# Normalising and transposing rows under the modulation weights' load, modulating three blocks at a time, and updating mLSTM states inside each head's projection

## The chip, the core and the metric

The kernel runs on one core of a Trainium2 chip. Its engines work side by side and meet through semaphores: TensorE (PE, with its weight loads listed as PEld), VectorE (DVE), ScalarE (ACT), GpSimd (POOL), and SyncE (SP), whose queue issues nearly all DMAs. The metric is the device time of one execution in microseconds, lower is better; a kernel's time is the median of several runs.

## The reference

One transformer layer over 128 context tokens (block 0) and 1024 latent tokens (blocks 1 to 8), width 1024. The layer reads attention and a bidirectional mLSTM from one input projection, merges them, and ends with a SwiGLU network. Everything is float32.

```python
def trunk_layer(x, mods, ...):
    sh1, sc1, g1, sh2, sc2, g2 = mods              # split of silu(cond) @ w_ada + b_ada
    h = rmsnorm(x, norm1_w) * (1 + sc1) + sh1
    aq, ak, av, mq, mk, mv, mo, mg = jnp.split(h @ w_in, SPLIT_POINTS, axis=-1)
    ...                                            # q/k norms, rotary
    attn_o = attention(aq, keys, vals)
    hm, st_f, st_b = mlstm_bidir(heads(mq), heads(mk) * (MLSTM_DK ** -0.5), heads(mv), gates, init_f, init_b)
    hm = (rmsnorm(hm, mlstm_norm_w) * jax.nn.sigmoid(mo))
    x = x + g1 * (jnp.concatenate([attn_o, hm], axis=-1) @ w_out)
    h2 = rmsnorm(x, norm2_w) * (1 + sc2) + sh2
    x = x + g2 * swiglu(h2, w_gu, w_down)

def step(carry, inp):                              # one mLSTM chunk of 128 tokens, per head and direction
    ...
    num = s @ vc + inter[..., None] * (qc @ C)
    C_new = decay[..., None, None] * C + jnp.einsum('bhs,bhsd,bhse->bhde', w, kc, vc)
    n_new = decay[..., None] * n + jnp.einsum('bhs,bhsd->bhd', w, kc)
```

The context rows are modulated with one condition and the latent rows with another. The latent scans start from given states; the context block starts from zero, and its states after one chunk are outputs.

## The kernel before

Tokens are nine blocks of 128 rows; three blocks form a chunk of 384 columns. A float32 operand is split into a high and a low part, so a product is three matmuls: high by high, high by low, low by high. The first projection uses float16 parts under a power-of-two scale that is taken from bounds on the features (`hsc`) and on the weights (`Scaled`).

The order that the code is written in is a list of priorities. A planner with a model of the engines' times orders each engine's instructions from it; `hot(n)` raises the priority of what stands in it. Generators are advanced against each other by `weave` (main against side steps) and `beside` (several sides, each with its own rate).

The stages, with their lines:

1. *Loads and modulation* (L265 to L377). SP's queue loads x block 0, then 16 pieces of the modulation weight (`aw`, 512 KB each). `strip_products` (L323) multiplies them with silu(cond); `cols_from_strips` (L329) turns the result into per-feature columns `shift1` and `scale1`. Both are then scaled per partition by `hsc` (L372 to L377). The key/value/gate columns of `w_in` (`kraw`, L444) and the other x blocks (L445 to L448) load after the modulation weights.
2. *Features* (L457 to L493). Per block: `normalise` (squares on ACT, reciprocal root in short DVE operations, scaling), eight transposes into PSUM (`transposed`, L344), then modulation straight from PSUM in eight 128x128 pieces (L470 on ACT, L473 on DVE) into float32 `full`; the high half is a cast (L479 on ACT, L481 on DVE), the low half a subtraction (L482, its instruction at L136, mostly on POOL). Side work: `ada`, the rest of the modulation weights, and `steps`, the bounds of the query weights.
3. *Keys, values, gates* (`linear_tok` with `evac_kvg`, L529), whose products the planner starts as features come.
4. *Query projection* (L965), with `gate_work` at rate 0.25, `ada` at 0.8, `kwork` at 0.8 and `steps` at 0.3 beside it. `gate_work` turns the gates into decay factors and the columns `QT` that the scans use; the part behind L579 waits ten side steps.
5. *Heads* (L1400 to L1405). `head_project(h)` makes queries (three chunks, L771) and then per block keys, values and output gates (L514 to L516, 384 columns; `evac` L749). `head_mlstm(h - 1)`, the scan of the head before, runs beside it at rate 0.67, attention at about 0.1. A scan first walks both directions in turn (L792 to L826): weight the values (`weighted`, POOL, on DVE in the last head), one 128x129 product with the keys (L813), one DVE update of the state (L823). Then it goes through the blocks (L847 to L890): products with queries and states (L834, L857, L864), a sum, a division by the normaliser (L867 to L878), and POOL multiplications (L881, L887).
6. *Last scan* (L1410), beside the first half of the output projection (`first`), the last modulation (`ada`) and attention.
7. Prefill, the feed-forward network and the finish follow (L1433 on).

## Time and profile before

| | us |
|---|---|
| median of 3 runs | 1625.65 |
| lowest and highest | 1624.38, 1627.73 |
| the profiled execution, its time | 1626.38 |
| the profiled execution, its span | 1624.6 |

The mean granted TensorE clock is 0.971 of full speed. The span is the time from the first to the last instruction of the profiled execution. A row of a group gives line, engine, operation, the output tile and its inputs, shapes and count, then the busy time and the mean time of one in ns, then the idle time of the engine just before them and what ended it. A row of the timeline gives start, duration, engine, line and operation, and in brackets the idle time before it and what released it. A row of the stages gives the stretch, its length, and per engine the busy time and the number of instructions, then the granted clock, the DMA engines' share and their rate. An instruction of PE that follows another closely overlaps it, so its duration is longer than its share of the engine.

### The profile page before, as it was taken

The page shows a single profiled execution, that of the slowest core. Times are in us where ns is not written, and L with a number is a line of the kernel's source. Part 1 is how long each engine was busy: PE and PEld are TensorE (multiplying, and loading weights), DVE is VectorE, ACT ScalarE, POOL GpSimd, SP SyncE. Part 2 cuts the span into 40 slices and gives each one's busy share as a digit, 9 for nine tenths or more (in the row PEclk, how much of TensorE's full clock was granted, in tenths as well). Part 3 has the DMA queues.
Part 4 walks back from the last instruction along what each step waited for, and adds up shares of the span by engine and source line. Part 5 has one row for each costly group of instructions (what it writes and reads, how often), then busy time and mean ns, then how long its engine had stood idle before and what let it go on. Part 6 is the DMA issues. An engine that isn't in the chain of part 4 may idle for free. (4 is left out here: it accounts for less than half of the span.)

```text
span 1624.6 us, 23438 instructions
## 1 busy us (share of the span) xinstructions
PE 1507.5 (93%) x8592; PEld 1254.6 (77%) x8592; DVE 937.6 (58%) x1895; ACT 755.6 (47%) x1373; POOL 657.5 (40%) x507
## 2 busy tenths in 40 slices
PE   5888899999988679999999999899999999999996
PEld 2644566667666467889999899798898989899995
DVE  3877745737657566556642646767674564333445
ACT  3754456756545444535433344565562443333232
POOL 0443332424241433544345354433434454545443
PEclk8899999999988899999999999999999999999998
DMA  9564232533447545867753546787774445545441
GB/s 356 184 178 128 83 71 49 112 50 66 103 108 175 184 141 124 211 167 169 174 153 114 149 146 212 188 181 170 163 171 131 132 142 173 157 130 149 129 142 68
DMA packets 387882, 236.92 MB, mean 146 GB/s; under 512 B 170199, under 2 KB 346791, under 8 KB 387767
## 3 DMA queue, kind: packets, MB, share of 16 engines
q1 hardware_dynamic: 385110, 231.84, 53.7%
q10 hardware_dynamic: 2656, 3.58, 0.7%
q8 instruction: 68, 1.11, 0.3%
q14 instruction: 48, 0.39, 0.1%
HBM read 183.79 MB, written 13.26 MB: 121 GB/s over the span
## 5 line engine op out<-in xcount | busy, mean ns | idle before, releaser
L136 POOL TENSOR_TENSOR wlo<-raw,whi 128x1024 fp32r<-128x1024 f32 (+1 forms) x144 | 352.0, 2448 | 419.3 <-ACT whi L153 387.9
L153 ACT CAST whi<-raw 128x1024 fp32r<-128x1024 f32 (+1 forms) x216 | 221.6, 1026 | 403.9 <-DMA raw<-in_w_gu_dram 160.4
L1305 PE MATMUL mm<-aTl,whi 128*128 128x384 f32 x1056 | 355.1, 336 | 0.0
L1304 PE MATMUL mm<-aTh,whi 128*128 128x384 f32 x1056 | 354.0, 336 | 0.9 <-DVE tn L1323 0.9
L1306 PE MATMUL mm<-aTh,wlo 128*128 128x384 f32 x1056 | 354.6, 336 | 0.0
L1304 PEld LDWEIGHTS mm<-aTh,whi 128*128 128x128 f32 x1056 | 198.2, 188 | 2.2 <-DVE tn L1323 1.5
L1306 PEld LDWEIGHTS mm<-aTh,wlo 128*128 128x128 f32 x1056 | 198.4, 188 | 1.5 <-issue 1.3
L1305 PEld LDWEIGHTS mm<-aTl,whi 128*128 128x128 f32 x1056 | 198.4, 188 | 0.8
L136 DVE TENSOR_TENSOR wlo<-raw,whi 128x1024 fp32r<-128x1024 f32 (+1 forms) x72 | 85.9, 1193 | 157.0 <-ACT whi L153 156.8
L514 PE MATMUL wi<-ipair,hT 128*128 128x384 f16 (+2 forms) x432 | 142.6, 332 | 9.8 <-ACT ipair L217 3.6
L515 PE MATMUL wi<-ipair,hT 128*128 128x384 f16 (+2 forms) x432 | 143.4, 332 | 4.3 <-DVE ipair L218 4.3
L1105 PE MATMUL mm<-wlo,hl 128*128 128x512 f32 x372 | 146.6, 395 | 0.0
L1104 PE MATMUL mm<-whi,hl 128*128 128x512 f32 x372 | 145.7, 396 | 0.7 <-ACT hl L1327 0.6
L1106 PE MATMUL mm<-whi,hl 128*128 128x512 f32 x372 | 143.7, 394 | 1.1 <-POOL hl L136 1.1
L516 PE MATMUL wi<-ipair,hT 128*128 128x384 f16 (+2 forms) x432 | 143.3, 332 | 0.2 <-POOL hT L136 0.2
L1031 DVE SCALAR_TENSOR_TENSOR pl<-pr,st,ph 128x1152 f16<-128x1152 f32 (+1 forms) x72 | 108.8, 1511 | 52.4 <-ACT ph L1030 50.5
L136 POOL TENSOR_TENSOR hl<-tn,hl 128x384 fp32r<-128x384 f32 x66 | 86.1, 1304 | 97.1 <-ACT hl L1327 97.1
L1027 ACT ACTIVATE pr<-S,st 128x1152 f32<-128x1152 f32 (+1 forms) x72 | 81.4, 1130 | 83.8 <-DVE st L1026 81.9
L1094 DVE TENSOR_TENSOR x<-x,t 128x512 f32<-128x512 f32 x102 | 116.2, 1161 | 0.8
L1323 DVE SCALAR_TENSOR_TENSOR tn<-tn,mm 128x384 f32<-128x384 f32 x66 | 36.4, 551 | 134.5 <-PE mm L1306 95.6
L1026 DVE TENSOR_REDUCE st<-S 128x1 f32<-128x1152 f32 (+1 forms) x72 | 88.8, 1233 | 25.5 <-PE S L1024 25.2
L1030 ACT ACTIVATE ph<-pr,st 128x1152 f16<-128x1152 f32 (+1 forms) x72 | 83.8, 1164 | 28.0 <-issue 8.1
(365 smaller groups left out, 2698.3 us busy)
## 6 DMA issues: line engine op xcount, KB each, us to landing
raw<-in_w_gu_dram SPq DMA_DIRECT2D x132, 512.0 KB
raw<-in_w_down_dram SPq DMA_DIRECT2D x60, 512.0 KB
a<-in_w_ada_dram SPq DMA_DIRECT2D x24, 512.0 KB
gl<-g_d SPq DMA_DIRECT2D x36, 256.0 KB
aw<-in_w_ada_dram SPq DMA_DIRECT2D x16, 512.0 KB
iraw<-in_w_in_dram SPq DMA_DIRECT2D x32, 256.0 KB
raw<-in_w_out_dram SPq DMA_DIRECT2D x12, 512.0 KB
x<-in_x_sample_dram SPq DMA_DIRECT2D x11, 512.0 KB
```

Source lines behind the costliest of these rows:

```text
L136: (dve if eng == "dve" else pool).tensor_tensor(out=out, in0=full, in1=hi, op=ALU.subtract)
L153: nc.scalar.copy(hi[:, :n], raw[:, :n])
L514: mm(ps[:, :n], ah, wh[:, k % 2, c0 : c0 + n], start=(k == 0), stop=False)
L515: mm(ps[:, :n], ah, wl[:, k % 2, c0 : c0 + n], start=False, stop=False)
L516: mm(ps[:, :n], al, wh[:, k % 2, c0 : c0 + n], start=False, stop=(k == KD - 1))
L1094: eng.tensor_tensor(out=x1[:, cs], in0=x1[:, cs], in1=t, op=ALU.add)
L1104: mm(ps, ah, wh[:, k % 2, :], start=(k == 0), stop=False)
L1105: mm(ps, ah, wl[:, k % 2, :], start=False, stop=False)
L1106: mm(ps, al, wh[:, k % 2, :], start=False, stop=(k == nk - 1))
L1304: mm(ps, wh[:, k, :], th[:, k, :], start=(k == 0), stop=False)
L1305: mm(ps, wh[:, k, :], tl[:, k, :], start=False, stop=False)
L1306: mm(ps, wl[:, k, :], th[:, k, :], start=False, stop=(k == KD - 1))
```

## The change

- x blocks 0 to 5 and the key/value/gate columns load ahead of the first modulation weights, blocks 6 to 8 behind them. x lives in three tiles of three blocks (`x3`).
- `normalise(c)` and `turn(c)` handle three blocks: after the scaling on DVE, the transposes go to PSUM and are copied back over x, half by ACT and half by DVE. Chunks 0 and 1 do this ahead of the modulation, chunk 2 between the products. The key/value/gate weights' scale and split come ahead of the modulation too, and no longer wait for `hsc`.
- `hsc` becomes one scale for all partitions, by a transpose, a maximum, and a product that spreads it (`power_scale`). The inverse scales are made later (`inverses`).
- `features(c)` modulates three blocks of one feature group at a time from SBUF: ACT writes the high half directly, DVE the float32 value, and the subtraction alternates between DVE and POOL. In chunk 0 the context block and the two others are separate instructions. Its products follow chunk by chunk.
- The bounds of weights write to SBUF instead of PSUM.
- In `head_project`, each block's `evac` ends with `update`: both directions' weighted values on POOL in one tile, one 258-column product, the forward state's update on DVE at once, and a copy of the backward part on ACT. `head_mlstm` begins with seven DVE updates for the backward direction. The key tile has 2 buffers instead of 9, `th` 1 instead of 2, the states 21 instead of 18; start states have tiles of their own.
- `gate_work` runs wholly beside the query projection. The rates of the side work change.

```diff
@@ -197,15 +198,18 @@
             t = gp.tile([P, 20], F32, name=nm("isc"), tag="isc", bufs=3)
             for j, raw in enumerate(raws):
                 for i in range(2):
-                    act(bank()[:, 0 : n // 2], raw[:, i * n // 2 : (i + 1) * n // 2], AF.Abs, accum_out=t[:, 12 + 2 * j + i : 13 + 2 * j + i])
+                    act(jkw[:, 0 : n // 2], raw[:, i * n // 2 : (i + 1) * n // 2], AF.Abs, accum_out=t[:, 12 + 2 * j + i : 13 + 2 * j + i])
                 yield
             dve.tensor_reduce(out=t[:, 4:5], in_=t[:, 12:20], axis=AX.X, op=ALU.max)
-            dve.tensor_tensor(out=t[:, 4:5], in0=t[:, 4:5], in1=hsc[:, 3:4], op=ALU.mult)
             yield from power_scale(gp, one1, t[:, 4:5], t[:, 6:8])
-            dve.tensor_tensor(out=t[:, 8:9], in0=t[:, 6:7], in1=hsc[:, 3:4], op=ALU.mult)
-            dve.tensor_scalar(out=t[:, 9:10], in0=t[:, 7:8], scalar1=P ** -0.5, scalar2=None, op0=ALU.mult)
-            dve.tensor_scalar(out=t[:, 10:11], in0=t[:, 7:8], scalar1=0.5, scalar2=None, op0=ALU.mult)
-            self.scale, self.inv, self.inv_k, self.inv_half = t[:, 8:9], t[:, 7:8], t[:, 9:10], t[:, 10:11]
+            self.t, self.scale = t, t[:, 6:7]
+        def inverses(self):
+            t = self.t
+            dve.tensor_tensor(out=t[:, 8:9], in0=t[:, 7:8], in1=hsc[:, 3:4], op=ALU.mult)
+            dve.tensor_scalar(out=t[:, 9:10], in0=t[:, 8:9], scalar1=P ** -0.5, scalar2=None, op0=ALU.mult)
+            dve.tensor_scalar(out=t[:, 10:11], in0=t[:, 8:9], scalar1=0.5, scalar2=None, op0=ALU.mult)
+            self.inv, self.inv_k, self.inv_half = t[:, 8:9], t[:, 9:10], t[:, 10:11]
@@ -270,14 +276,29 @@
-    xs = [p0.tile([P, D], F32, name=f"x{b}") for b in range(NB)]
-    dma(xs[0], xrow(0))
+    x3 = [p0.tile([P, CB, D], F32, name=f"x3_{c}") for c in range(NCH)]
+    def load_x(b):
+        dma(x3[b // CB][:, b % CB], xrow(b))
+    def rows_of(j):
+        return w_in[2 * j * P : (2 * j + 2) * P, :].rearrange("(a p) n -> p a n", p=P)
+    for b in range(2 * CB):
+        load_x(b)
+    kvg = Scaled([[(lambda v: v[:, :, 0:256], rows_of(j)[:, :, 512:768]),
+                   (lambda v: v[:, :, 256:272], rows_of(j)[:, :, 2816:2832])] for j in range(4)], (2, 272),
+                 [p0.tile([P, 544], F32, name=f"kraw{j}") for j in range(4)])
+    kvg_steps = kvg.ready()
+    next(kvg_steps)
     ada_w = [[], []]
     for n in range(2):
         for k in range(KD):
             aw = awp.tile([P, D], F32, name=f"aw0_{n}_{k}")
             dma(aw, w_ada[k * P : (k + 1) * P, n * D : (n + 1) * D])
             ada_w[n].append(aw)
+    for b in range(2 * CB, NB):
+        load_x(b)
@@ -329,52 +350,60 @@
...
+    def normalise(c):
+        ssx = p0.tile([P, CB], F32, name=f"ssx{c}")
+        for i in range(CB):
             jk = p0.tile([P, D], BF16, name=nm("jk"), tag="jk", bufs=2)
+            act(jk, x3[c][:, i], AF.Square, accum_out=ssx[:, i : i + 1])
+        rs = rsqrt(p0, ssx, CB, 1.0 / D)
+        for i in range(CB):
+            dve.tensor_scalar(out=x3[c][:, i], in0=x3[c][:, i], scalar1=rs[:, i : i + 1], scalar2=None, op0=ALU.mult)
+    def turn(c):
+        for i in range(CB):
+            x = x3[c][:, i]
+            pss = []
+            for half in range(2):
+                ps = bank()
+                for j in range(4):
+                    k = half * 4 + j
+                    transpose(ps[:, j * P : (j + 1) * P], x[:, k * P : (k + 1) * P])
+                pss.append(ps)
+            nc.scalar.copy(x[:, 0:512], pss[0])
+            dve.tensor_copy(x[:, 512:1024], pss[1])
+    for c in range(2):
+        normalise(c)
+        turn(c)
+    emit(kvg_steps)
+    kvg_pairs = kvg.pairs(1)
...
+        with hot(300):
+            for j, pe in enumerate(halves):
+                part = p0.tile([P, 512], F32, name=nm("part"), tag="part", bufs=2)
+                (nc.scalar.copy if j == 0 else dve.tensor_copy)(part, pe)
+                cols_from_strips(out, n, j, part, bankA)
...
-    dve.tensor_reduce(out=hs2, in_=shift1, axis=AX.XY, op=ALU.max, apply_absolute_value=True)
-    dve.tensor_reduce(out=hsc[:, 0:1], in_=scale1, axis=AX.XY, op=ALU.max, apply_absolute_value=True)
-    dve.scalar_tensor_tensor(out=hsc[:, 0:1], in0=hsc[:, 0:1], scalar=float(D) ** 0.5, in1=hs2, op0=ALU.mult, op1=ALU.add)
-    powers(hsc, P)
-    for t in (scale1, shift1):
-        dve.tensor_scalar(out=t, in0=t, scalar1=hsc[:, 2:3], scalar2=None, op0=ALU.mult)
+    with hot(300):
+        dve.tensor_reduce(out=hs2, in_=shift1, axis=AX.XY, op=ALU.max, apply_absolute_value=True)
+        dve.tensor_reduce(out=hbd, in_=scale1, axis=AX.XY, op=ALU.max, apply_absolute_value=True)
+        dve.scalar_tensor_tensor(out=hbd, in0=hbd, scalar=float(D) ** 0.5, in1=hs2, op0=ALU.mult, op1=ALU.add)
+        emit(power_scale(gp, one1, hbd, hsc[:, 2:4]))
+        for t in (scale1, shift1):
+            dve.tensor_scalar(out=t, in0=t, scalar1=hsc[:, 2:3], scalar2=None, op0=ALU.mult)
+        kvg.inverses()
@@ -454,52 +472,6 @@
-    for c in range(NCH):
...
-            for half, ps in enumerate(xT[b] if b < 1 else transposed(b)):
-                full = p0.tile([P, 4, P], F32, name=nm("full"), tag="full", bufs=3)
...
-            if b >= 3:
-                for _ in range(3):
-                    next(ada)
...
@@ -526,12 +498,46 @@
...
+    def features(c):
+        v = x3[c].rearrange("p b (k x) -> p k b x", k=KD)
+        hh, hl = (t[c].rearrange("p k (b x) -> p k b x", b=CB) for t in (hTh, hTl))
+        for k in range(KD):
+            full = p0.tile([P, CB, P], F32, name=nm("full"), tag="full", bufs=4)
+            for i, n in ((0, 1), (1, 2)) if c == 0 else ((0, CB),):
+                cnd = 0 if n == 1 else 1
+                s, t = scale1[:, k, cnd : cnd + 1], shift1[:, k, cnd : cnd + 1]
+                act(hh[:, k, i : i + n], v[:, k, i : i + n], AF.Identity, scale=s, bias=t)
+                dve.tensor_scalar(out=full[:, i : i + n], in0=v[:, k, i : i + n], scalar1=s, scalar2=t, op0=ALU.mult, op1=ALU.add)
+            sub(hl[:, k], full, hh[:, k], "dve" if k % 2 == 0 else "pool")
+    for c in range(NCH):
+        with hot(100):
+            features(c)
+        prods = linear_tok(kvg_pairs, 0, 272, evac_kvg, (tuple(range(c * CB, c * CB + CB)),), bank if c == 1 else bankA)
+        if c > 0:
+            weave(prods, chain(steps, ada), KD, 10)
+        else:
+            emit(prods)
+        if c == 0:
+            normalise(2)
+        if c == 1:
+            turn(2)
+    emit(steps)
...
@@ -741,18 +747,19 @@
...
+        w.inverses()
...
-            kt = mlp.tile([P, P], F32, name=nm("kt"), tag="kt", bufs=MB)
+            kt = mlp.tile([P, P], F32, name=nm("kt"), tag="kt", bufs=2)
...
-            th = mlp.tile([P, P], F32, name=nm("th"), tag="th", bufs=2)
+            th = mlp.tile([P, P], F32, name=nm("th"), tag="th", bufs=1)
@@ -761,7 +768,40 @@
             transpose(pt[:, 0:P], kt)
             kT = mlp.tile([P, P], F32, name=nm("kT"), tag="kT", bufs=MB)
             nc.scalar.copy(kT, pt[:, 0:P])
-            st["b"][b] = (kT, kt, va, so)
+            st["b"][b] = (kT, va, so)
+            update(b, kt, va)
+        st["s"] = states = {}
+        st["raw"] = raws = {}
+        for d in range(2):
+            c0 = mlp.tile([P, P + 1], F32, name=nm("c0"), tag=("c0f", "c0b")[d], bufs=2 - d)
+            dma(c0[:, 0:P], I["state_C"][0, 0, d, h])
+            dma(c0[:, P : P + 1], I["state_n"][0, 0, d, h].rearrange("(p o) -> p o", o=1))
+            states[d, 1 if d == 0 else NBL] = c0
+        def update(b, kt, va):
+            wv = mlp.tile([P, 2, P + 1], F32, name=nm("wv"), tag="wv", bufs=2)
+            for d in range(2):
+                pool.tensor_tensor(out=wv[:, d], in0=va, in1=qcol(1, d, b, h).to_broadcast([P, P + 1]), op=ALU.mult)
+            pc = bank()
+            mm(pc[:, 0 : 2 * (P + 1)], kt, wv.rearrange("p d x -> p (d x)"), start=True, stop=True)
+            for d in range(2):
+                if b == (NBL if d == 0 else 1):
+                    continue
+                add = pc[:, d * (P + 1) : (d + 1) * (P + 1)]
+                cn = mlp.tile([P, P + 1], F32, name=nm("cs"), tag="cs", bufs=CSB)
+                if d == 0 and b > 0:
+                    dve.scalar_tensor_tensor(out=cn, in0=states[0, b], scalar=decb[:, b * 4 + h : b * 4 + h + 1], in1=add,
+                                             op0=ALU.mult, op1=ALU.add)
+                    states[0, b + 1] = cn
+                    continue
+                nc.scalar.copy(cn, add)
+                if b > 0:
+                    raws[b] = cn
+                    continue
+                dma(O["new_state_C"][0, 0, d, h], cn[:, 0:P])
+                dma(O["new_state_n"][0, 0, d, h].rearrange("(p o) -> p o", o=1), cn[:, P : P + 1])
         def q_group(cs):
             banks = [bankA() for _ in cs]
@@ -787,43 +827,12 @@
...
-            def weighted(b):
...
-            for j, b in enumerate(seq):
-                wv = ahead.pop(0)
...
+        blocks, states = st["b"], st["s"]
+        for b in range(NBL, 1, -1):
+            col = 64 + b * 4 + h
+            dve.scalar_tensor_tensor(out=st["raw"][b], in0=states[1, b], scalar=decb[:, col : col + 1], in1=st["raw"][b],
+                                     op0=ALU.mult, op1=ALU.add)
+            states[1, b - 1] = st["raw"][b]
@@ -960,9 +969,11 @@
     gates = gate_work(mlp)
     sts = [{} for _ in range(NH)]
     w_q = groups_in[0].pairs()
+    groups_in[0].inverses()
     steps = groups_in[1].ready()
     next(steps)
-    weave(linear_tok(w_q, 0, 512, evac_q(qp, qcc, qss, qw)), beside((gates, 0.25), (ada, 0.8), (kwork, 0.8), (steps, 0.3)), 40, 40)
+    weave(linear_tok(w_q, 0, 512, evac_q(qp, qcc, qss, qw)), beside((gates, 0.7), (ada, 1.15), (kwork, 0.6), (steps, 0.3)), 40, 40)
+    emit(gates)
     emit(steps)
     groups_in[1].made = groups_in[1].pairs()
     emit(ada)
@@ -1397,17 +1408,16 @@
-    weave(head_project(0, sts[0]), beside((gates, 0.3), (att, 0.1)), 96, 96)
-    emit(gates)
+    weave(head_project(0, sts[0]), beside((att, 0.1),), 96, 96)
         scan = head_mlstm(h - 1, sts[h - 1])
-        weave(head_project(h, sts[h]), beside((scan, 0.67), (att, 0.11)), 96, 96)
+        weave(head_project(h, sts[h]), beside((scan, 0.42), (att, 0.11)), 96, 96)
     scan = head_mlstm(NH - 1, sts[NH - 1])
-    weave(scan, beside((ada, 0.35), (first, 0.25), (att, 0.1)), 57, 57)
+    weave(scan, beside((ada, 0.5), (first, 0.35), (att, 0.14)), 37, 37)
```

124 lines of the change are left out of this document (14 added, 110 removed).

## The prediction

> **What bounds the kernel now.** I read the page first, for the shares of the engines, then busy time by stage, then the timeline where stages meet, then groups of instructions inside the stages that the change touches.
>
> ```profile
> span 1624.6 us, 23438 instructions
> ...
> PE 1507.5 (93%) x8592; PEld 1254.6 (77%) x8592; DVE 937.6 (58%) x1895; ACT 755.6 (47%) x1373; POOL 657.5 (40%) x507
> ```
>
> TensorE (PE) is busy 93% on average, but the change lies in the first third alone, so I cut that third where the PE timeline changes its product: features and key/value/gate projection (about 36 to 94 us), query projection (to 170), head 0 (to 228), heads 1 to 3, each beside the scan of the head before it, and the last scan (468 to 552).
>
> ```profile
> core 0: us, PE busy (x) PEld busy (x) DVE busy (x) ACT busy (x) POOL busy (x), PEclk, DMA share, GB/s
> 0.00:36.00 36.00, 22.36 (x108) 8.09 (x108) 9.38 (x50) 9.86 (x28) 1.07 (x7) 0.87 0.96 349
> 36.00:94.00 58.00, 48.52 (x387) 33.72 (x388) 46.68 (x160) 40.47 (x92) 21.00 (x19) 0.87 0.63 202
> 94.00:170.00 76.00, 64.84 (x366) 29.58 (x364) 57.14 (x156) 38.51 (x67) 31.70 (x23) 0.96 0.50 150
> 170.00:228.00 58.00, 54.50 (x328) 33.70 (x327) 33.60 (x110) 26.75 (x78) 19.23 (x32) 0.94 0.17 49
> 228.00:310.00 82.00, 76.05 (x497) 54.60 (x495) 48.85 (x119) 55.11 (x146) 26.65 (x50) 1.00 0.37 75
> 310.00:388.00 78.00, 74.73 (x508) 54.08 (x507) 41.43 (x119) 44.84 (x132) 26.04 (x54) 1.00 0.40 66
> 388.00:468.00 80.00, 76.29 (x525) 57.16 (x523) 48.04 (x127) 46.04 (x126) 26.56 (x56) 1.00 0.52 114
> 468.00:552.00 84.00, 64.58 (x376) 48.32 (x375) 63.67 (x170) 40.00 (x101) 29.82 (x31) 0.88 0.55 131
> ```
>
> The reader is to see four regimes. Until 36 us the DMA share is 0.96: the weights' arrival bounds. Until 94 us DVE is busy 46.68 of 58, and PE's 48.52 includes matmuls that drain while nothing follows. In heads 0 to 3 PE is busy 93 to 96%. In the last scan PE falls to 64.58 of 84 and DVE, at 63.67, is as busy as PE: a chain between the two.
>
> **The change part by part.** (1) *Loads.* Five more x blocks (5 x 0.524 MB) and the k/v/gate columns (1024 x 272 x 4 B, 1.11 MB) go ahead of the 16 modulation weights on SP's queue.
>
> ```profile
> GB/s 0 62 177 366 408 407 419 248 331 342 404 422 415 411 415 408 411 411 415 411 411 408 371 317 287 282 200 392 375 411 408 419 426 415 401 397 406 406 410 413
> ...
> 26.95 1.05 PE L323 MATMUL wi<-aw,silp 128*32 128x512 f32 x4 [0.29 <-DMA aw<-in_w_ada_dram]
> ...
> 34.92 0.41 DVE L473 TENSOR_SCALAR full<-mm,scale,shift 128x128 f32<-128x128 f32 x1
> ...
> 39.97 0.38 PE L514 MATMUL wi<-ipair,hT 128*128 128x272 f16 x1 [2.90 <-ACT ipair L217]
> ...
> 93.68 0.59 PE L514 MATMUL wi<-ipair,hT 128*128 128x512 f16 x2 [0.71 <-ACT ipair L217]
> ```
>
> The first row is the DMA rate of the first 45 us in 40 slices of 1.13 us: a plateau near 410 GB/s, dented to 200 to 317 in the slices in which the narrow k/v/gate columns load. 3.73 MB at 410 is 9.1 us; the dent (about 0.67 MB missing over five slices) adds 1.6. The last strip product, 26.95 before, moves to about 37.7. From there to the first modulated tile took 8.0 us; about 2.9 of it DVE stood at the weights' maximum, which is now done earlier, and the new common scale puts one transpose, six short DVE operations and one product (about 2.6 us, as the same chain for the weights takes) in its place. The first modulated tile comes at about 45.4 instead of 34.9: **10.5 us later**. Normalising, turning and splitting behind it hide under the weights' DMA, where DVE works 9.38 of 36 us; without that cover they would cost their DVE time.
>
> (2) *Features.* Between 34.92 and 93.68 (58.8 us) the change works on these groups of DVE and ACT:
>
> ```profile
> L473 DVE TENSOR_SCALAR full<-mm,scale,shift 128x128 f32<-128x128 f32 x44 | 15.6, 402 | 2.3 <-PE mm L115 1.1 <-ACT full L470 1.1
> L481 DVE CAST hT<-full 128x512 f16<-128x512 f32 x9 | 5.2, 578 | 0.9 <-ACT full L470 0.9
> L340 DVE TENSOR_SCALAR x<-x,ry 128x1024 f32<-128x1024 f32 x5 | 3.5, 750 | 0.0
> L136 DVE TENSOR_TENSOR hT<-full,hT 128x512 f16<-128x512 f32 x3 | 2.7, 885 | 0.7 <-ACT hT L479 0.5
> ...
> L470 ACT ACTIVATE full<-mm,shift,scale 128x128 f32<-128x128 f32 x26 | 11.4, 459 | 4.8 <-DVE full L473 4.6 <-PE mm L115 0.2
> ...
> L479 ACT CAST hT<-full 128x512 f16<-128x512 f32 x9 | 5.5, 617 | 3.0 <-DVE full L473 3.0
> ```
>
> DVE loses these 27.0 us, some 12 of short reciprocal-root operations (two of three sets move under the loads) and 1.6 of weight splits: 40.6. It gains 24 modulations over 384 columns (the first chunk's in two pieces): 402 ns for 128 from PSUM and 750 ns for 1024 from SBUF bound one at 0.28 to 0.75; I take 0.38, with 0.53 for the two pieces, 10.3 in all. Twelve subtractions at 0.55 add 6.6 and block group 2 (norm, copies) 6.4. So 46.7 becomes about 30. ACT goes from 40.5 to about 30 too: 11.4 and 5.5 go, with half of the squares, one scaling of x and the weight splits (about 14, all under the loads now), and 24 modulations come at 0.5 to 0.9 (one 128 wide took 459 ns, one 512 wide 617) and block group 2's squares and copies (some 5). What speaks against it:
>
> ```profile
> 8.11 0.16 DVE L132 SCALAR_TENSOR_TENSOR ry<-rt,ry 128x1 f32<-128x1 f32 x1
> ...
> 38.51 2.26 POOL L136 TENSOR_TENSOR hT<-full,hT 128x512 f16<-128x512 f32 x2 [27.50 <-DVE rt L131]
> 38.54 1.15 DVE L132 SCALAR_TENSOR_TENSOR ry<-rt,ry 128x2 f32<-128x2 f32 x1
> ```
>
> A 0.16 us operation took 1.15 beside a POOL subtraction. The modulations read PSUM now and SBUF afterwards, so 12 POOL subtractions (0.9 us each, from 1.13) could each hold DVE: 0 to 11 us. I add 3. The Trainium skill, "SBUF — State Buffer", Who interferes with whom, says that a DVE instruction in a two-port mode or with two SBUF inputs and a GpSimd instruction exclude each other for their whole length, while one that reads PSUM goes free; the row agrees, and by that rule the sum would take nearly the full 11.
>
> 33 us at the same DVE share (46.68 of 58) is 41 us: the first query product at 45.4 + 41 = 86.4 instead of 93.7, **-7**. Bounds: DVE packed without a gap, 78 (-15); the old length kept, 104 (+10).
>
> (3) *Gates.* Their second half must now end ahead of head 0, so it moves into the query stage.
>
> ```profile
> 173.35 0.27 DVE L585 COPY be<-mm 1x128 f32<-1x128 f32 x1
> ...
> 206.59 0.68 DVE L651 COPY QT<-mm 128x512 f32<-128x512 f32 x1
> ```
>
> These are the first and last of 35 DVE operations, 11.6 us. DVE has 19 us free in the query stage, so 0 if they fit the gaps, 15 if its share (57.14 of 76) stays. The gates are a chain with few long operations; I take **+4**, nearer to 0. The modulation units pushed back here (some four) ride on ACT, busy 38.51 of 76; without that cover 1 us each.
>
> (4) *State updates beside the projection.*
>
> ```profile
> 462.49 0.61 PE L857 MATMUL mm<-cs,qT 128*128 128x129 f32 x4
> ...
> L802 POOL TENSOR_TENSOR wv<-va,QT 128x129 f32<-128x129 f32 x16 | 6.2, 398 | 15.4 <-PE mm L813 14.3 <-ACT va L753 1.0
> ...
> L823 DVE SCALAR_TENSOR_TENSOR cs<-cs,decb,mm 128x129 f32<-128x129 f32 x14 | 4.9, 350 | 11.7 <-PE mm L813 10.8
> L753 ACT ACTIVATE va<-wi,isc 128x128 f32<-128x128 f32 x9 | 3.3, 369 | 1.4 <-PE mm L864 1.3
> ```
>
> A 129-wide float32 product is two instructions, 0.11 us apart: 0.22. Sixteen per head (3.5 us) become nine of 258 columns at about 0.44 (4.0). POOL weights 18 times instead of 16 and ACT copies nine results (0.37 each, 3.3 us, busy 55 of 82 at most). Head 0 gets 4.0 of PE and loses 1.5 of gates: **+2**. In heads 1 to 3 PE is idle 5.95 + 3.27 + 3.71 = 12.9 us; the chain product, DVE, product that opened each scan goes, but DVE, ACT and attention chains stay. From -12 to +1: **-4**. New waits: PE stands at an update until POOL's weights come, and behind it are the next block's 24 matmuls; two key buffers instead of nine make ACT wait for that update in turn. On SP's queue the start states and the new states of a head move forward with it, into the projection, where its DMA share is 0.37 to 0.52. The backward start state has one buffer, which the old scan's last block frees, so its load is late and the seven remaining DVE steps of the next scan wait for it, as they did once before:
>
> ```profile
> DVE cs L823 <- DMA cs<-in_state_n_dram: 1.9, 1, 1.9
> ```
>
> That is 2 us of DVE per head, with softmax and evacuations behind it; it was there before and stays, so it costs 0.
>
> (5) *Last scan.*
>
> ```profile
> 475.28 0.28 DVE L804 TENSOR_SCALAR wv<-va,QT 128x129 f32<-128x129 f32 x1
> ...
> 506.19 0.34 DVE L823 SCALAR_TENSOR_TENSOR cs<-cs,decb,mm 128x129 f32<-128x129 f32 x1
> ...
> 507.78 0.75 DVE L842 TENSOR_TENSOR sd<-mm,dt 128x256 f32<-128x256 f32 x2
> ...
> 475.00:508.00 33.00, 22.97 (x108) 16.77 (x109) 21.96 (x53) 10.35 (x17) 7.89 (x6) 0.69 0.70 138
> 508.00:552.00 44.00, 35.85 (x224) 27.01 (x222) 35.95 (x107) 24.48 (x69) 15.38 (x17) 1.00 0.46 128
> ...
> L804 DVE TENSOR_SCALAR wv<-va,QT 128x129 f32<-128x129 f32 x14 | 5.7, 415 | 4.4 <-PE mm L813 4.4
> ...
> L813 PE MATMUL mm<-wv,kt 128*128 128x129 f32 x32 | 8.7, 397 | 7.4 <-DVE wv L804 4.6 <-DVE cs L818 1.2 <-DVE cs L823 0.9
> ```
>
> From 475.3 to 506.2 the scan only updates states; its blocks begin at 507.8. Now seven DVE steps of 0.35 (2.5 us) remain, so blocks could begin near 479: -29 if nothing else lay there. DVE's 21.96 of 33 hold 5.7 of weighting, 4.8 of updates and 0.6 of copies; the other 11 (attention, the end of head 2's scan, half the output projection, the last modulation) must go beside the blocks. At their stretch's share (35.95 of 44) that takes 13.4 us: 33 - 13.4 - 2.5 = **-17**. Least is -9, what DVE drops, if every idle gap stays. What is late next: that side work and its DMAs.
>
> Sum: -7 + 4 + 2 - 4 - 17 = -22. The profiled execution took 1626.38 us, 1.8 beyond its span and 0.7 above the median 1625.65 of the runs. 1626.4 - 22 = 1604.4; against the median, 1603.7. I say **1604**. From the prefill on nothing is edited.
>
> **Rivals.** (A) *Slower: PE waits for POOL at every update.* A POOL instruction in the scan already stands for ACT:
>
> ```profile
> L881 POOL TENSOR_TENSOR hm<-hm,so 128x128 f32<-128x128 f32 x10 | 5.5, 552 | 17.4 <-ACT jkh L880 17.3
> ```
>
> That is 1.7 us each; an update's weights behind it hold PE. There are 36 updates, so 0.6 us each (22 / 36) eats the gain and 1 us gives 1604 + 36 = 1640. For it: engines run in order. Against: weights were on POOL in heads 1 to 3 before, with PE 93 to 96% busy. (B) *The lock.* POOL's subtractions hold DVE for the full 11, the modulated tiles start 10.5 late and gates fill DVE: features +2, gates +8, rest as forecast: 1617. (C) *The change does not do what it says in the tail:* side work sets the last scan's length, only DVE's 9 go: 1612. (D) *More:* blocks start at once (-27) and the idle of the heads goes (-10): 1588.
>
> **How the numbers follow.** Forecast (1596 to 1610) 0.45, A 0.09, B 0.15, C 0.13, D 0.18. About 0.2% (3.3 us) is what measuring this kernel can tell from no change. Below 1622 lie the forecast, C, D and two thirds of B: faster 0.86; same 0.05, the upper third of B; slower 0.09, A. The range 1582 to 1623 leaves out A and the far end of D.
>
> **What would show it.** First modulated tile near 45 us, first query product near 86, head 0 beginning near 167, heads 1 to 3 at 77 to 80 us each, the last scan near 67 us with no gap before its first block. It is wrong if PE waits at the 258-wide update for POOL, if short DVE operations stretch to 1 us throughout the features, or if the query stage passes 85 us.

## The result, and the profile after

The changed kernel took 1605.09 us (median of 4 runs, 1599.83 to 1606.1) against 1625.02 for the kernel before in the same session (4 runs, 1621.53 to 1627.73): a ratio of 0.9872, 95% interval 0.9843 to 0.9901. The forecast was 1604, its range 1582 to 1623.

The head of the page after, and the stages cut from its trace (stretch, length, busy time and instructions of each engine, granted clock, DMA share, rate):

```profile
span 1604.4 us, 23368 instructions
...
PE 1502.1 (94%) x8539; PEld 1252.0 (78%) x8539; DVE 929.7 (58%) x1856; ACT 767.1 (48%) x1409; POOL 658.9 (41%) x526
```

```profile
47.00:89.00 42.00, 36.04 (x280) 24.90 (x281) 32.80 (x85) 31.07 (x67) 13.38 (x13) 0.85 0.43 136
89.00:170.00 81.00, 71.40 (x445) 34.02 (x443) 66.86 (x214) 40.85 (x77) 32.20 (x25) 0.97 0.58 164
170.00:234.00 64.00, 59.11 (x334) 36.39 (x333) 27.74 (x83) 26.50 (x81) 26.69 (x46) 0.90 0.24 45
234.00:319.00 85.00, 79.15 (x494) 57.53 (x492) 53.50 (x126) 60.78 (x166) 29.51 (x59) 0.94 0.44 86
319.00:392.00 73.00, 71.27 (x476) 51.35 (x475) 35.52 (x102) 43.09 (x123) 23.54 (x50) 1.00 0.31 61
392.00:468.00 76.00, 74.13 (x501) 54.44 (x500) 46.74 (x120) 45.20 (x130) 28.47 (x57) 1.00 0.58 111
468.00:527.00 59.00, 47.08 (x301) 35.52 (x300) 46.42 (x119) 36.86 (x92) 27.00 (x29) 0.94 0.56 148
```

The rows are features, query projection, heads 0 to 3 and last scan. The last scan is short now. But head 0, which is only a projection with some attention beside it, takes 64 us at a clock of 0.90, and head 1 takes 85 at 0.94.

Both kernels were profiled a second time. The table cuts each trace at the first product of a stage (the last scan ends at the last query-key product of the last head):

| length, us | before | before again | after | after again | predicted change | measured, 1st and 2nd pair |
|---|---|---|---|---|---|---|
| to the first query product | 93.7 | 92.7 | 89.0 | 87.4 | -7 | -4.7, -5.4 |
| query stage | 76.6 | 76.6 | 80.8 | 80.8 | +4 | +4.2, +4.2 |
| head 0 | 58.2 | 59.3 | 64.1 | 63.1 | +2 | +5.9, +3.8 |
| heads 1 to 3 | 238.8 | 237.5 | 234.1 | 234.2 | -4 | -4.7, -3.3 |
| last scan | 75.5 | 75.9 | 59.1 | 60.4 | -17 | -16.4, -15.5 |
| to the first product of the feed-forward network | 110.9 | 112.8 | 115.0 | 113.3 | 0 | +4.1, +0.5 |
| from there to the end | 970.9 | 966.9 | 962.3 | 963.8 | 0 | -8.6, -3.1 |
| span | 1624.6 | 1621.7 | 1604.4 | 1602.9 | -22 | -20.2, -18.8 |

The sum was nearly right, and part of that is luck: the five rows that were priced give -15.7 and -16.2 instead of -22, and the two rows that were priced at nothing bring -4.5 and -2.6 more. The cut between the first two rows also misleads. In the first profile after, the first query product stands alone among the key/value/gate products, and the next one begins 3.7 us later:

```profile
88.95 0.38 PE L486 MATMUL wi<-ipair,hT 128*128 128x512 f16 x1
89.17 0.28 PE L488 MATMUL wi<-ipair,hT 128*128 128x272 f16 x1
...
92.53 0.28 PE L488 MATMUL wi<-ipair,hT 128*128 128x272 f16 x1
92.64 0.38 PE L487 MATMUL wi<-ipair,hT 128*128 128x512 f16 x1
```

In both profiles after, 30 key/value/gate products (the 272 columns), 3.5 us of PE, come behind the first query product; in the kernel before none does. So 3.5 us of the first row's gain are moved into the second row, where they make up most of the +4.2. Head 0 begins at 169.8 and 168.1 us instead of 170.3 and 169.3: the two stages together gain 0.5 and 1.2 us, and not 3.

**Where head 0 loses its time.** SP's queue, ACT and PE in head 0 of the changed kernel (start, duration, engine, line, operation; in brackets the idle time before it and what ended it):

```profile
195.58 0.34 SPq L803 DMA_DIRECT2D out_new_state_C_dram<-cs  x1
195.97 0.42 SPq L804 DMA_DIRECT2D out_new_state_n_dram<-cs  x1
196.69 0.80 SPq L732 DMA_DIRECT2D q_d<-qraw  x2
197.58 0.41 SPq L803 DMA_DIRECT2D out_new_state_C_dram<-cs  x1
198.04 0.45 SPq L804 DMA_DIRECT2D out_new_state_n_dram<-cs  x1
...
207.05 0.37 ACT L1038 ACTIVATE pr<-S,st 128x128 f32<-128x128 f32 x1 [9.15 <-DMA q_d<-qraw]
...
207.56 0.69 PE L1035 MATMUL S<-kst,qT 128*128 128x128 f32 x2 [4.89 <-ACT pr L1038]
```

The softmax tile `pr` lies over the freed `qraw`, so its first writer waits until the last two `q_d` writes have landed. They were issued at 196.69, and ACT was released near 207. The DMA view of 192 to 210 us shows what went on meanwhile (40 slices of 0.45 us: busy tenths of the DMA engines, where a packet that has begun counts as busy until it ends, then what they moved):

```profile
DMA  0000000001407999028197993108000000000003
GB/s 0 0 0 0 0 0 0 0 0 36 110 1 269 387 387 156 3 9 6 1 18 17 11 16 13 1 6 7 5 0 0 0 0 0 0 0 0 0 0 73
```

From 200 to 205 us the engines are busy at up to 0.9 while they move 1 to 18 GB/s. By the packet records of the trace, the 2 KB packets of `q_d` had ended by 201.1; the 512-byte and 4-byte packets around and behind them ran until 206.4, single ones for up to 3.3 us. Among the writes of this time are the two of `new_state_n`, 128 elements of 4 bytes each, which the change moved from the scan into the projection. ACT stands for 9.15 us, PE for 4.89 behind it, and then the clock falls (0.90 in this stage).

### The profile page after: what moved, and what is told of

Its sections match the earlier page's. It is cut to its first block, busy times and chain, and to the rows that moved or that the text cites. A ratio compares the mean times of both kernels' runs of the same rounds, so it can differ in the third digit from the quotient of the medians.

```text
span 1604.4 us, 23368 instructions
## 1 busy us (share of the span) xinstructions
PE 1502.1 (94%) x8539; PEld 1252.0 (78%) x8539; DVE 929.7 (58%) x1856; ACT 767.1 (48%) x1409; POOL 658.9 (41%) x526
## 5 line engine op out<-in xcount | busy, mean ns | idle before, releaser
L486 PE MATMUL wi<-ipair,hT 128*128 128x384 f16 (+2 forms) x408 | 138.7, 341 | 2.6 <-DVE G L499 1.2
L1042 DVE SCALAR_TENSOR_TENSOR pl<-pr,st,ph 128x1152 f16<-128x1152 f32 (+1 forms) x72 | 107.3, 1491 | 55.6 <-ACT ph L1041 50.7
L487 PE MATMUL wi<-ipair,hT 128*128 128x384 f16 (+2 forms) x408 | 138.2, 339 | 1.3 <-DVE ipair L222 1.3
L488 PE MATMUL wi<-ipair,hT 128*128 128x384 f16 (+2 forms) x408 | 136.5, 340 | 1.7 <-DVE hT L137 1.7
L1035 PE MATMUL S<-kst,qT 128*128 128x384 f32 (+1 forms) x400 | 88.8, 351 | 5.4 <-ACT pr L1038 5.3
```

What stands on the lines that cost most here:

```text
L486: mm(ps[:, :n], ah, wh[:, k % 2, c0 : c0 + n], start=(k == 0), stop=False)
L487: mm(ps[:, :n], ah, wl[:, k % 2, c0 : c0 + n], start=False, stop=False)
L488: mm(ps[:, :n], al, wh[:, k % 2, c0 : c0 + n], start=False, stop=(k == KD - 1))
```

## Experiments

**Do the two profiles repeat?** No edit.

> The kernel before, profiled a second time. Theory 1 (the 8.5 us that the change gained inside the unedited feed-forward stage belong to the kernels): the stall of 3.2 us at po (L1049) for the transposed probabilities near 700 us and the half clock of 6.8 us behind it come again, the product 96 of the gate_up group ends near 740 us as in the first profile, span within 3 us of 1624.6. Theory 2 (an event of one execution): no such stall, feed-forward 6 to 9 us shorter, span near 1616.

> The changed kernel, profiled a second time. Theory 1 (head 0 pays for its own state outputs): ACT waits about 9 us at the softmax tile pr (L1038) for the last q_d writes near 198 to 207 us, PE about 5 behind it, a half clock of 6.8 us follows, and head 0 takes 64 us again. Theory 2 (one execution's luck on the DMA rings): the wait is near the 1.4 us that it was before, and head 0 takes 58 to 60 us.

Measured: the table above; times 1623.5 and 1604.67. Head 0's wait came again: ACT idle for 8.59 us, PE for 4.79 behind it. The stall in the feed-forward network came again too. PE's waits around the end of its first group in the first profile of before:

```profile
PE po L1049 <- DMA plT<-pl: 3.2, 1, 3.2
```

(total, times, longest). Before again it was 3.0; in the changed kernel it is absent once and 1.3 the other time. Over all kernels of this study it is 1.9 to 3.2 with the old scans and at most 1.4 with the new ones. So some 2 to 3 us there do come with the change, although no line of that stage is edited; why the transposed probabilities land in time is not shown. The half clock of 6.8 us behind that stall in the first profile of before did not come in the second; that part is one execution's.

**The front alone, and the heads alone.** In the first, head_project, head_mlstm, their tiles, the gates' rate and the rates of L1411 to L1420 are those of before; in the second, everything ahead of them and the bounds' PSUM banks.

```diff
--- changed kernel
+++ front alone
-    weave(linear_tok(w_q, 0, 512, evac_q(qp, qcc, qss, qw)), beside((gates, 0.7), (ada, 1.15), (kwork, 0.6), (steps, 0.3)), 40, 40)
-    emit(gates)
+    weave(linear_tok(w_q, 0, 512, evac_q(qp, qcc, qss, qw)), beside((gates, 0.25), (ada, 1.15), (kwork, 0.6), (steps, 0.3)), 40, 40)
...
--- before
+++ heads alone
-    weave(linear_tok(w_q, 0, 512, evac_q(qp, qcc, qss, qw)), beside((gates, 0.25), (ada, 0.8), (kwork, 0.8), (steps, 0.3)), 40, 40)
+    weave(linear_tok(w_q, 0, 512, evac_q(qp, qcc, qss, qw)), beside((gates, 0.7), (ada, 0.8), (kwork, 0.8), (steps, 0.3)), 40, 40)
+    emit(gates)
...
```

> Only loads, normalising, turning, modulation and the common scale are changed; heads, scans, gates' rate in the query stage and the rates of side work in heads and last scan are those of before. Theory 1 (parts add): first query product near 89, head 0 begins 4 to 5 us earlier than before (166), the rest as before: 1620 to 1622, ratio 0.997 to 0.998. Theory 2 (the front's gain is lost to a later wait): 1625, ratio 1.000. Theory 3 (the 8.5 us in the feed-forward stage come from the front's shift in time): about 1612, ratio 0.992.

> Only the heads, scans, gates' rate and the rates of heads and last scan are changed; loads, normalising and modulation are those of before. Theory 1 (parts add): query stage +4, head 0 +6, heads 1 to 3 -5, last scan -16, the way to the feed-forward network +4, and -8 in it: 1610 to 1612, ratio 0.991. Theory 2 (without the feed-forward's gain): 1618, ratio 0.996. Theory 3 (the front's early features are needed for the gates to end in time): above 1620.

Measured: the front alone 1608.46 (0.991, 0.9891 to 0.9929), the heads alone 1601.58 (0.987, 0.9853 to 0.9887). No theory had that: the halves are worth 14.7 and 21.6 us against the 1623.14 of that session, 36 together, and both at once bring about 20. The front alone reaches the first query product at 86.7 (with the same 30 products behind it) and head 0 at 166.6, 2.7 to 3.7 us earlier than before, but it also has heads 0 and 1 of 55.6 and 75.3 us instead of 59.3 and 80.7, which no edit of loads or features touches. In before, PE stood in head 0 for a query evacuation; PE, and DVE just ahead of it, in before again:

```profile
179.83 2.22 DVE L616 TENSOR_TENSOR dec<-Mp,Me 1x128 f32<-1x128 f32 x1
...
182.63 0.48 PE L771 MATMUL wi<-hT,ipair 128*128 128x384 f16 x1 [3.90 <-DVE qT L777]
```

A one-row gate operation took 2.22 us, and a queue of gate steps held the evacuation. In the front alone the same steps fall elsewhere and PE waits for none of it; in the heads alone the gates are done before head 0. Either half removes this stall, and together they cannot remove it twice. That accounts for about 4 of the 16 us. By stages, the second profile of after against before again, the gain that is missing from the sum of the halves is 3.8 us in head 0, 7.9 in heads 1 to 3 and 5.5 on the way to the feed-forward network; the other stages give some 4 back.

**The 4-byte writes.** Three edits of the changed kernel: without the writes of new_state_n; as rows; and both state writes on ACT's queue.

```diff
--- changed kernel
+++ as rows
                 dma(O["new_state_C"][0, 0, d, h], cn[:, 0:P])
-                dma(O["new_state_n"][0, 0, d, h].rearrange("(p o) -> p o", o=1), cn[:, P : P + 1])
+                new_n.append(cn)
+                if d == 1:
+                    pr_ = bank()
+                    for e in range(2):
+                        transpose(pr_[0:1, e * P : (e + 1) * P], new_n[e][:, P : P + 1])
+                    nrow2 = mlp.tile([P, 2, P + 1], F32, name=nm("wv"), tag="wv", bufs=2)[0:1, :, 0:P]
+                    nc.scalar.copy(nrow2, pr_[0:1, 0 : 2 * P].rearrange("p (e x) -> p e x", e=2))
+                    for e in range(2):
+                        dma(O["new_state_n"][0, 0, e : e + 1, h], nrow2[:, e])
--- changed kernel
+++ on ACT's queue
-                dma(O["new_state_C"][0, 0, d, h], cn[:, 0:P])
-                dma(O["new_state_n"][0, 0, d, h].rearrange("(p o) -> p o", o=1), cn[:, P : P + 1])
+                nc.scalar.dma_start(O["new_state_C"][0, 0, d, h], cn[:, 0:P])
+                nc.scalar.dma_start(O["new_state_n"][0, 0, d, h].rearrange("(p o) -> p o", o=1), cn[:, P : P + 1])
```

> The changed kernel without the eight writes of new_state_n (that output is left out). Theory 1 (the 4-byte elements of these writes hold the DMA rings, so that q_d's writes land about 9 us after their issue, the softmax tile waits and PE with it): q_d's last writes land 2.5 to 3 us after their issue, the ACT wait of 9 us at pr (L1038) and the PE wait of 4.8 behind it are gone, head 0 takes 55 to 58 us instead of 63 to 64, whole kernel 6 to 8 us faster. Theory 2 (the 64 KB state matrices or the queue's order cause it): ACT still waits 6 us or more and head 0 stays above 61.

> The changed kernel, but new_state_n goes out as rows: two transposes of a column on PE per head, one ACT copy, two writes of one 512-byte packet each. Theory 1 (4-byte elements): as without these writes, less 0.5 us of PE per head: 1597 to 1600, ratio to before 0.984 to 0.986. Theory 2 (state matrices or queue order): 1604 to 1606, no better than the changed kernel.

> The changed kernel, but the new states leave through ACT's queue instead of SP's, with the same 4-byte elements. Theory 1a (the elements hold the DMA engines, whichever queue they come from): q_d still lands 6 us or more after its issue, ACT waits at pr, 1603 to 1606. Theory 1b (only what stands behind them on the same queue waits): q_d lands in 3 us, head 0 takes 56 to 58, 1597 to 1600.

Measured: 1593.72 without (one run); as rows 1590.87 (0.9797, 0.9775 to 0.982); on ACT's queue 1602.67 (0.9875, 0.9852 to 0.9897). The first theories hold by their waits, and the times came out lower than they said. The same ACT instruction in the three, in that order:

```profile
196.69 0.37 ACT L1037 ACTIVATE pr<-S,st 128x128 f32<-128x128 f32 x1 [1.62 <-DMA q_d<-qraw]
```

```profile
198.23 0.37 ACT L1048 ACTIVATE pr<-S,st 128x128 f32<-128x128 f32 x1 [0.79 <-DMA q_d<-qraw]
```

```profile
203.50 0.37 ACT L1038 ACTIVATE pr<-S,st 128x128 f32<-128x128 f32 x1 [9.19 <-DMA q_d<-qraw]
```

With the elements gone or packed, the wait is gone, with the state matrices still around the `q_d` writes on SP's queue; with the elements on the other queue it is the same 9.2 us. So it is the elements, and not the order on the queue or the matrices. The packet records of the run with ACT's queue say what `q_d` suffers: its 2 KB packets take 0.09 us in the median and up to 5.46; with rows none takes more than 0.11. They also say that the elements are over by then: their last packet ends at 193.92, each took about 0.01, and the first packet of `q_d` begins at 193.98; the slow ones begin at 195.05 and the last ends at 202.31. The Trainium skill, "DMA: Bandwidth & Descriptors", Queues, rings and completion order, has each DMA engine serve its queues in turn, a packet from each. This run doesn't test that, since no packet of the elements was left to take turns with; whatever slows `q_d` outlasts their packets.

The stages with rows (query stage, heads 0 to 3, last scan):

```profile
88.70:169.00 80.30, 72.34 (x445) 34.61 (x443) 65.24 (x210) 40.75 (x77) 31.64 (x25) 0.96 0.57 163
169.00:224.20 55.20, 55.20 (x335) 35.30 (x335) 28.20 (x84) 26.96 (x81) 26.60 (x46) 0.97 0.18 53
224.20:301.70 77.50, 72.43 (x465) 51.64 (x463) 45.01 (x108) 54.20 (x151) 27.11 (x52) 1.00 0.34 80
301.70:379.00 77.30, 75.57 (x509) 54.90 (x508) 44.66 (x121) 50.65 (x142) 25.18 (x59) 1.00 0.32 72
379.00:455.70 76.70, 74.75 (x505) 54.34 (x503) 45.54 (x118) 45.68 (x129) 28.37 (x57) 1.00 0.49 110
455.70:514.20 58.50, 47.36 (x301) 35.50 (x300) 46.00 (x120) 36.90 (x95) 26.90 (x29) 0.94 0.56 149
```

PE is busy for all of head 0, 55.2 us, 7.9 less than in the second profile of after; heads 1 to 3 together lose 2.7. That loss isn't shown to come from the elements, for without their writes heads 1 to 3 take 234.4 us, head 1 still 85.2, and head 0 takes 55.8. The version with rows beats both kernels: 14 us below the changed one by the medians, 12 by the ratios, whose intervals do not meet.

**Did the elements cost as much where they stood?** The kernel before, with rows (one transpose, one ACT copy and one 512-byte packet per direction and head, in the scan).

> The kernel before, with new_state_n written as rows (one transpose, one ACT copy and one packet per direction and head). Theory 1 (the 4-byte elements only hurt where the change put them, in head 0 ahead of the last q_d writes): 1622 to 1627, ratio 0.998 to 1.002. Theory 2 (they cost as much where they stood, in the scans): 1609 to 1614, ratio 0.991 to 0.993.

Measured: 1629.46 against 1621.56 (1.0038, 1.0023 to 1.0052), a little above the first theory. Rows are slower there; heads 1 to 3 take 242.7 us instead of 237.5. So the elements cost the kernel before nothing that rows would save; they became a cost where the change put them. Packets were slow there too: in the last scan the 1 KB packets take up to 5.70 and 5.12 us in the two profiles before, and at most 0.86 with rows. No longer time of the kernel follows from it, so what counts is whether the path waits for such a landing.

**The bounds' PSUM banks.** One edit of the change put alone into before, and taken back in after.

```diff
-                    act(bank()[:, 0 : n // 2], raw[:, i * n // 2 : (i + 1) * n // 2], AF.Abs, accum_out=t[:, 12 + 2 * j + i : 13 + 2 * j + i])
+                    act(jkw[:, 0 : n // 2], raw[:, i * n // 2 : (i + 1) * n // 2], AF.Abs, accum_out=t[:, 12 + 2 * j + i : 13 + 2 * j + i])
```

> The kernel before with one edit of the change alone: the weights' bounds write their absolute values to SBUF instead of a PSUM bank. The front alone made heads 0 and 1 shorter by 3.7 and 5.4 us, which no edit of the loads or features reaches. Theory 1 (the bounds' banks stood in the way of PE's transposes and scans): heads 0 and 1 together 5 to 9 us shorter, 1614 to 1618, ratio 0.995. Theory 2 (it was the order of the gate work at head 0, shifted by the front's timing): within 2 us of before, ratio 0.999 to 1.001.

> The changed kernel with one edit undone: the weights' bounds write their absolute values to a PSUM bank again. In the kernel before this edit alone was worth 5.5 us. Theory 1 (it is a part of the change's gain that the prediction did not cost): 1608 to 1612, ratio to before 0.990 to 0.992, the query stage 3 to 5 us longer. Theory 2 (inside the change it is worth nothing, since other waits take its place): 1602 to 1606, ratio 0.987.

Measured: alone 1619.52 (0.997, 0.9958 to 0.9983), a gain of 5.5 us. Heads 0 and 1 are 3.8 shorter together, less than the first theory's 5; the larger part lies in the query stage, 71.3 us instead of 76.6, which neither theory named, and some is given back later. Taken back in the changed kernel: 1599.32 (0.9854, 0.9835 to 0.9874), below both theories, the interval overlapping that of the changed kernel. So inside the change this edit is worth nothing that these runs can tell. Head 0 keeps a stall of 4.3 us for `pr` there.

**Is the front worth anything beside the new heads?** The heads alone, with rows.

> Only heads, scans and rates of the change, with new_state_n as rows; loads, features and the bounds' banks are those of before. With element writes the heads and scans alone took 1601.6, the whole change 1605.1, so the front seemed to be worth nothing. Theory 1 (the 4-byte writes hid the front's gain; without them the parts add): 1598 to 1602, 8 to 12 above the whole change with rows (1590.9). Theory 2 (the front is worth nothing beside the new heads): 1588 to 1592.

Measured: 1593.51 against 1621.56 (0.983, 0.9813 to 0.9846); the whole change with rows has 0.9797. By the ratios the front adds 0.33%, 5 us, with intervals that just meet: between the two theories. It reaches the first query product 3.7 us earlier (88.7 against 92.4), with the 30 products behind it, its query stage is 1.0 longer, and head 0 begins 2.7 earlier.

**The lock between DVE and POOL in the features.** The version with rows, all 24 subtractions on DVE.

```diff
-            sub(hl[:, k], full, hh[:, k], "dve" if k % 2 == 0 else "pool")
+            sub(hl[:, k], full, hh[:, k], "dve")
```

> The changed kernel with new_state_n as rows, and all 24 subtractions of the features on DVE, none on POOL. In the changed kernel a DVE subtraction takes 0.55 us alone and 0.90 beside a POOL one. Theory 1 (the lock is worth about as much as the moved work: 12 x 0.55 = 6.6 us more DVE, 12 x 0.35 = 4.2 less of stretch): first query product 1 to 3 us later, 1590 to 1594. Theory 2 (the lock is the bound of the features, as the rival had it: 11 us): first query product 3 to 5 us earlier, 1586 to 1589.

Measured: 1601.77 (0.9877, 0.986 to 0.9894), 11 slower than with the shared work, which neither theory had. The stage itself got shorter, from 43.0 to 39.7 us; the two stretches from first key/value product to first query product, shared and on DVE alone:

```profile
45.70:88.70 43.00, 36.21 (x280) 24.84 (x281) 33.38 (x87) 31.18 (x67) 13.39 (x13) 0.84 0.47 141
```

```profile
46.70:86.40 39.70, 33.44 (x279) 23.39 (x280) 33.37 (x92) 30.83 (x66) 0.00 (x0) 0.92 0.47 148
```

DVE's busy time is the same with 12 subtractions more: what it saves in waiting for POOL pays for a part of them. By its groups the shared version spends 2.9 us more in the smaller modulations (7.2 against 6.2), one step of the reciprocal root (1.9 against 0.5) and the stretched subtractions (0.60 against 0.56 each). The stretch is 3.3 us shorter on DVE alone, 1.9 when it is counted to the last key/value/gate product, and the clock is higher in it. So the lock and the handing over cost 2 to 3 us here. The loss is in the next stages, which the edit does not name: the query stage takes 83.3 instead of 80.3, head 0 64.0 instead of 55.2, with one stall that the shared version has not:

```profile
181.01 0.69 PE L1045 MATMUL S<-kst,qT 128*128 128x128 f32 x2 [6.06 <-DVE qT L137]
```

There the eight bounds of a head's weights stand on ACT in one row ahead of the attention's query casts, which come at 178.26; with the shared work the casts come between the bounds, at 169.39 and 172.48. An edit of the features changed the order 100 us later.

## Why the prediction held, step by step

(1) *Loads.* The last four strip products began at 38.69 and 37.21 (37.7 said, counted like the 26.95), the first modulated tile at 46.38 and 44.54 (45.4). Right.

(2) *Features: a step that failed.* The row says -4.7 and -5.4 instead of -7, but 3.5 us of that are products that only changed their place. The last key/value/gate product begins at 92.5 and 90.9 us, against 91.3 and 90.1 before: not earlier at all. The step took the length of the stretch from DVE's share alone and left out PE, whose products start later now and are as many: between the first and the last of them PE is busy 39.7 of 45.7 us and DVE 35.8, and PE's longest wait in all there is 3.8 for a load of the modulation weights. DVE's groups after:

```profile
L511 DVE TENSOR_SCALAR full<-x,scale,shift 128x384 f32<-128x384 f32 x16 | 10.0, 662 | 0.2 <-POOL hT L137 0.2
L137 DVE TENSOR_TENSOR hT<-full,hT 128x384 f16<-128x384 f32 x12 | 7.1, 604 | 0.0
...
L511 DVE TENSOR_SCALAR full<-x,scale,shift 128x256 f32<-128x256 f32 x8 | 3.8, 477 | 0.0
L511 DVE TENSOR_SCALAR full<-x,scale,shift 128x128 f32<-128x128 f32 x8 | 3.4, 427 | 0.0
```

On DVE the mis-sized term is the modulation from SBUF: 0.66 us for 384 columns, not 0.38, so 17.2 us in all instead of 10.3. It had been scaled by width from 0.75 for 1024 columns, and even 128 take 0.34 here. DVE's busy time came to 32.8 where the step had 30 and 3 for the lock; that this agrees with a term too small by 6.9 is luck, in part because instructions overlap (modulations that follow one another begin 0.58 us apart). The +3 for the lock fits the 2 to 3 of the last experiment. From the Trainium skill's rule ("SBUF — State Buffer", Who interferes with whom) the prediction worked out nearly 11, an estimate in which every modulation is held. The trace has the rule's effect on single instructions, 1.06 us for 128 columns and 1.00 for 256 beside a POOL subtraction instead of 0.34 and 0.40, but not that sum: the 384-column modulations take 0.66 beside POOL, and 0.65 to 0.70 in the run that has no POOL subtraction.

(3) *Gates, +4.* With the old front and the gates moved (the heads alone) the query stage is 80.5, so for the gates the size was right there. With the new front and the gates' second half left in head 0 (the front alone) it was already 79.9: that is the 3.5 us of key/value/gate products, and other side work besides. Both together cost 4.2 and not 7, so that the row of the changed kernel agrees is luck; how the two make room for each other is not shown. Part of the front's share is what the step named as the missing cover: modulation units pushed back from the features. PE's strips in the query stage, before again and after:

```profile
L323 PE MATMUL mm<-a,silp 128*32 128x256 f32 x96 | 8.5, 411 | 0.0
```

```profile
L344 PE MATMUL mm<-a,silp 128*32 128x256 f32 x128 | 9.8, 390 | 0.0
...
L453 PE MATMUL mm<-part,strip_sel 128*2 128x512 f32 x2 | 1.0, 592 | 0.0
```

They are on PE, not on ACT alone, so PE's own work grew. The front also has the bounds' edit, which alone made this stage 5.3 us shorter; how the two go together was not taken apart.

(4) *State updates.* Heads 1 to 3 -4.7 and -3.3 (-4 said). Head 0 +5.9 and +3.8 instead of +2: **the step that failed most.** It said that the new states move forward on SP's queue, into a projection where the DMA share is 0.37 to 0.52, and gave that no price. With the elements packed head 0 is 55.2 and without them 55.8, that is 2 to 4 us shorter than before rather than 2 longer. The step also left out that PE's stall behind the gates, 3.5 and 3.9 us in head 0 before, would go with them. In the whole kernel the unpriced writes cost 11 to 14 us (1605.1 against 1593.7 without them and 1590.9 as rows). That heads 1 to 3 sum up right hides 85, 73 and 76 us where 77 to 80 each were forecast.

(5) *Last scan.* -16.4 and -15.5 (-17 said): right in size. What ends PE's longest wait there is DVE, whose side work was to set the stage; PE's wait from head 0 on (in all, times, longest; 5.1 of it in the last scan):

```profile
PE mm L873 <- DVE sd L851: 5.4, 3, 4.8
```

No run took this term apart. Part was given back on the way to the feed-forward network (+4.1, +0.5), and 2 to 3 us came in it, as above.

*Rivals.* (A) fell: the one wait of PE at the 258-wide update is for ACT, and POOL's weighting waits for ACT's values, not PE for POOL. PE's waits from head 0 to the last scan, and POOL's group in heads 1 to 3:

```profile
PE mm L788 <- ACT it L869: 0.3, 1, 0.3
```

```profile
L786 POOL TENSOR_TENSOR wv<-va,QT 128x129 f32<-128x129 f32 x53 | 21.5, 427 | 32.0 <-ACT va L760 31.9
```

(B) fell by the size of the lock and the query stage, (C) by the last scan. Of (D), blocks that start at once did not come: the last scan has -16.4 and -15.5, not -27. Idle time of PE in heads 1 to 3, 12.9 us before, is 8.8 with rows, so 4 us went and not 10. That the version with rows comes close to the 1588 of (D) is therefore chance.

What stays open: why 4-byte writes slow other packets; and, of the 16 us by which the halves do not add, all but the stall for the query evacuation. With rows the gap is smaller (15 and 28 alone by their ratios, 33 together), so part of it may have been the elements. The rest was not pinned to an instruction.

## What to carry to other kernels

When a step moves, list its DMAs with the size of their smallest contiguous piece, and ask which landing the path waits for near their new place: here eight writes of 512 bytes in 4-byte pieces, harmless to the time in the scans, cost 11 to 14 us in the projections, most of it beside a buffer that was about to be reused. Write columns as rows where they meet such a wait, and leave them where they do not. Where a planner orders the engines, the parts of a change do not add: judge a part by its own stage and by the stalls in the next one, not by the difference of two totals. And see that a cut between stages falls where the work of one is done: a first product can run ahead of it.

## What was unexpected in the hardware

After 4-byte elements were written, the DMA engines were busy for about 5 us at 1 to 18 GB/s, and 2 KB packets of another queue took up to 5.46 us instead of 0.09, although the elements' own packets took 0.01 and were over. Reads suffer as well: in head 1 of the changed kernel the read back of `q_d` on ACT's queue began 2.0 us after the last state packet had ended at 263.2, and its 2 KB packets took up to 6.80 us; with rows none took more than 0.55. And DVE and POOL hold each other up in the heads too: in the second profile after, at the end of head 1, a DVE weight split that had taken 1.28 us took 3.00 beside a POOL split of 2.12, and PE stood 2.30 behind it:

```profile
298.22 1.28 DVE L222 SCALAR_TENSOR_TENSOR ipair<-iraw,isc,ipair 128x1024 f16<-128x1024 f32 x1
...
304.18 3.00 DVE L222 SCALAR_TENSOR_TENSOR ipair<-iraw,isc,ipair 128x1024 f16<-128x1024 f32 x1
```

```profile
303.98 2.12 POOL L137 TENSOR_TENSOR ipair<-iraw,ipair 128x1024 f16<-128x1024 f32 x1
```
